# Two operand sums cut when they are made, and residual and SBUF corrections added by accumulating DMAs, in the MLP of a hybrid decoder block on one core

## The chip, the cores and the metric

The kernel runs on one core of a Trainium2 chip. The metric is the device time of one execution in microseconds (us), as the median of three runs. PE is the matrix engine, DVE the vector engine, ACT the scalar engine, POOL and SP issue DMAs here. The granted clock is the share of its full 2.4 GHz that TensorE was allowed in a stretch; its other level is 1.2 GHz.

## The reference, cut to what matters

```
h = x + mixer_block(rmsnorm(x))              # S5 branch and short convolution, gated, projected
xn = rmsnorm(h)                              # xn: 1024 features x 1024 positions
a = relu(xn @ w_ff1)                         # 4096 features
h = h + (a * a) @ w_ff2                      # the squared-ReLU MLP
return rmsnorm(h)
```

All is float32. The change touches only the MLP and the residual sum of its last line.

## The kernel before, in words

**Products.** Each float32 operand is cut into a high part (ACT copies it to fp32r) and a low part (DVE subtracts the high part), and a product is three matmuls: high by high, high by low, low by high. Both layers of the MLP are mostly done in groups of seven products (Strassen's scheme in Winograd's form) in place of eight. `seven(g, after)` (L1196) is one group: chains P1, then P4 of the group before (`last_product`, L1243), P5, P2, P6, P3, P7, each of 12 matmuls. Its four results come out of the chains P2 (c11), P3 (c12), P7 (c22) and, a group later, P4 (c21); `done` (L1231) takes them out of PSUM. P4 continues the accumulation in the bank `seed` in which P7 ended, so it can't start before DVE has read c22 from that bank. c12 and c22 each need a correction, `v2` and `s5`, which ACT copies out of PSUM in the middle of the group.

**Stages.** 14 groups of W1 (g = 0 to 13), 16 plain products `pf` of W2 (slab 6), 12 groups of W2 (g = 14 to 25: three chunks q of four groups e), then the last slab of W2 in plain products with the last normalisation.

**Operands of W2.** From g = 2 on each W1 group computes its activations c11, c12, c22, c21 and the sums that the scheme needs of them: t1, t3, n2, t4. POOL stores them to DRAM (`xd`), 256 KB each, seven per group. Before the W2 chunk that needs them, SP loads them (`x_load`, L1177: two loads of 512 KB for each of seven operands B11, t1, B21, n2, B22, t3, t4) and `x_cut` (L1185) cuts each load, with a 128x1024 copy on ACT and a 128x1024 subtraction on DVE (recorded at L930).

**Weights.** `group_load` loads two blocks per group; `w_parts` makes sums (s1, s2 on DVE), highs (h0 to h3 on ACT) and lows (l0 to l3 on DVE). The plan `FIRST` (L1073, W1) or `SECOND` (W2) says behind which chain, `after(i)`, each is written.

**Order.** The order of every engine's queue is the order of the code: what `after(i)` writes stands behind chain i's evacuation. A late instruction holds up all behind it on its engine. SP runs its loads in order, POOL its stores.

**Residual.** `h` after the mixer was stored to DRAM (`hd`, eight blocks of 128x1024). After the W1 groups SP loads the eight blocks into `ha` (L1314), and DVE adds each product of W2 to them: L1330 for `pf`, L1237 in the groups, and a second instruction there, L1239, subtracts v2 or s5.

**End of W2.** During the final group (g = 25) the last slab (`fl`, `slab_cut`) and four weight blocks (`lw`, `cut`) are cut, in turn, at after(2) to after(6).

Of the kernel before, what the change touches and what calls it, by code (L numbers as in the profile page):

```python
# [45 lines left out]
def block_kernel(ctx, tc, x_t, par, ssm, w_u, win, wco, wglu, wo, w1, w2, out):
# [632 lines left out]
    def ssm_z():  # L679
# [34 lines left out]
        (q, nm): dram.tile([P, 4, HALF], F32, tag=f"xd{q}{nm}", name=f"xd{q}{nm}")  # L714
        for q in range(N_CHUNK) for nm in X_OF.values()
# [357 lines left out]
    FIRST = ["s1 h0", "s2 h1 l0", "h2 l1", "l2"], ["", "", "h3", "l3"]  # L1073
# [103 lines left out]
    def x_load(q, name):  # L1177
        ts = []
        for u in range(2):
            t = unit(f"xl{q}{name}{u}", F32R)  # L1180
            nc.sync.dma_start(t.bitcast(F32), xd[q, name][:, 2 * u:2 * u + 2, :].rearrange("p k t -> p (k t)"))
            ts.append(t)
        xq[q, name] = ts
# [15 lines left out]
    def seven(g, after):  # L1199
# [10 lines left out]
        s5, v2 = half(f"s5_{g}"), half(f"v2_{g}")  # L1210
        A.activation(s5, pe, AF.Copy)
# [5 lines left out]
        A.activation(v2, seed, AF.Copy)  # L1217
# [14 lines left out]
    def done(g, quad, ps, less):  # L1232

        i, hh = int(quad[1]) - 1, int(quad[2]) - 1
        if g >= N_GROUP:
            y = h[2 * ((g - N_GROUP) % 4) + i][:, HS[hh]]
            V.tensor_add(y, ps, y)  # L1237
            if less is not None:
                V.tensor_sub(y, y, less)  # L1239
# [4 lines left out]
        def out_of(name, t):  # L1244
            nc.gpsimd.dma_start(xd[q, name][:, c, :], t)
# [74 lines left out]
    for j in range(16):  # L1320
# [10 lines left out]
        if j % 2 and j < 12:
            x_load(0, names_x[j // 2])
            if j > 1:
                x_cut(0, names_x[j // 2 - 1])
# [152 lines left out]
```

## Time and profile before

| | |
|---|---|
| time, median of 3 runs | 1485.74 us (1485.54 to 1486.83) |
| the profiled execution's own time | 1487.28 us |
| its span, first to last instruction | 1485.5 us |
| PE busy | 1450.2 us, 98% of the span |
| DVE busy | 1008.4 us, 68% |
| ACT busy | 545.1 us, 37% |
| POOL busy | 131.3 us, 9% |
| mean granted clock | 0.991 |
| one chain of 12 matmuls, back to back | 2.72 us |
| one group of seven | 19.04 us |

PE is the engine to look at: it has work for nearly the whole span, so time can only be won where it stands idle or where its clock is low. Both happen in few places, so the table of totals says little; the waits of PE say which instruction ended each stop, the timeline says where that instruction stood in its queue, and the windows say what clock followed.

### The profile page before, as it was taken

How to read it: one execution, taken by the hardware profiler on the slowest of the kernel's cores; microseconds unless marked ns; L12 is line 12 of the kernel's file. 1: busy time of each engine (PE TensorE's matmuls, PEld its weight loads, DVE VectorE, ACT ScalarE, POOL GpSimd, SP SyncE). 2: the span in 40 equal slices, each digit the busy share in tenths (PEclk: the TensorE clock that was granted, in tenths of full speed). 3: DMA queues.
4: the chain of work that ended last, by engine and by line, in shares of the span. 5: the costliest groups of instructions: out<-in, count | busy, mean ns of one | idle time of the engine just before them, and what ended most of it. 6: DMA issues, size and time to landing. Idle time of an engine off the chain costs nothing.

```text
span 1485.5 us, 16929 instructions
## 1 busy us (share of the span) xinstructions
PE 1450.2 (98%) x6563; PEld 1200.9 (81%) x6563; DVE 1008.4 (68%) x1573; ACT 545.1 (37%) x776; POOL 131.3 (9%) x306
## 2 busy tenths in 40 slices
PE   9989999999999999999999999999999999998997
PEld 7868888888888888888888878888887787887887
DVE  6678487776877776347536866766666657767565
ACT  6541432223232238324213443333324224344354
POOL 5840000000000000000010001222111000000000
PEclk9999999999999999999999999999999999999999
DMA  5111111101111111114312233444458516162302
GB/s 215 29 43 43 43 43 50 48 32 56 43 43 43 43 43 35 65 57 156 135 43 94 78 105 123 153 156 148 151 169 347 169 53 232 57 217 94 114 28 87
DMA packets 44096, 144.31 MB, mean 97 GB/s; under 512 B 5488, under 2 KB 9968, under 8 KB 44016
## 3 DMA queue, kind: packets, MB, share of 16 engines
q1 hardware_dynamic: 34736, 112.82, 22.6%
q0 software_dynamic: 9280, 30.42, 5.3%
q8 instruction: 51, 0.84, 0.2%
q14 instruction: 29, 0.24, 0.1%
HBM read 108.61 MB, written 34.60 MB: 96 GB/s over the span
## 4 chain that ended last, share of the span: by engine, by line
PE 83%; DVE 9%; ACT 4%; DMA 2%; issue 2%; SPq 0%; DVEq 0%; ACTq 0%
PE ps L134 8%; PE ps L136 8%; PE ps L135 8%; PE seed L1088 4%; PE seed L1090 4%; PE seed L1089 4%; PE pa L1090 3%; PE pa L1089 3%; PE pa L1088 3%; PE pe L1090 3%; PE pe L1089 3%; PE pe L1088 3%; PE pc L134 2%; PE pg L136 2%; PE pg L135 2%; PE pc L136 2%
## 5 line engine op out<-in xcount | busy, mean ns | idle before, releaser
L134 PE MATMUL ps<-xh,wh 128*128 128x512 f32 x656 | 259.8, 396 | 1.2 <-ACT wh L94 1.2
L136 PE MATMUL ps<-xh,wl 128*128 128x512 f32 x656 | 256.1, 390 | 2.2 <-DVE wl L95 2.2
L135 PE MATMUL ps<-xl,wh 128*128 128x512 f32 x656 | 255.3, 389 | 0.0
L136 PEld LDWEIGHTS ps<-xh,wl 128*128 128x128 f32 x656 | 123.1, 188 | 29.8 <-DVE wl L95 3.9
L134 PEld LDWEIGHTS ps<-xh,wh 128*128 128x128 f32 x656 | 123.3, 188 | 28.6 <-ACT wh L94 2.3
L135 PEld LDWEIGHTS ps<-xl,wh 128*128 128x128 f32 x656 | 123.2, 188 | 25.3
L95 DVE TENSOR_TENSOR wl<-wr,wh 128x1024 fp32r<-128x1024 f32 x57 | 70.1, 1230 | 59.0 <-ACT wh L94 59.0
L94 ACT ACTIVATE wh<-wr 128x1024 fp32r<-128x1024 f32 x57 | 59.6, 1047 | 52.3 <-PE pc L135 21.0
L1204 ACT ACTIVATE seed<-pa 128x512 f32<-128x512 f32 x26 | 15.1, 582 | 160.2 <-PE pa L1090 160.2
L893 POOL DMA_DIRECT2D hd<-h x16 | 8.9, 559 | 711.5 <-ACT ssum L895 636.4
L1060 DVE TENSOR_TENSOR gl<-gs,gh 128x1024 fp32r<-128x1024 f32 x52 | 63.3, 1219 | 0.0
L1056 ACT ACTIVATE gh<-gs 128x1024 fp32r<-128x1024 f32 x52 | 54.7, 1052 | 22.5 <-DVE gs L1052 11.7
L134 PE MATMUL pc<-vh,wh 128*128 128x512 f32 x128 | 49.9, 390 | 0.0
L134 PE MATMUL pw<-mh,hwo 128*128 128x512 f32 x128 | 49.9, 390 | 0.0
L136 PE MATMUL pc<-vh,wl 128*128 128x512 f32 x128 | 49.8, 389 | 0.0
L136 PE MATMUL pw<-mh,lwo 128*128 128x512 f32 x128 | 49.8, 389 | 0.0
L135 PE MATMUL pw<-ml,hwo 128*128 128x512 f32 x128 | 49.8, 389 | 0.0
L134 PE MATMUL pg<-zh,wh 128*128 128x512 f32 x128 | 49.8, 389 | 0.0
L135 PE MATMUL pg<-zl,wh 128*128 128x512 f32 x128 | 49.8, 389 | 0.0
L136 PE MATMUL pg<-zh,wl 128*128 128x512 f32 x128 | 49.8, 389 | 0.0
L135 PE MATMUL pc<-vl,wh 128*128 128x512 f32 x128 | 49.8, 389 | 0.0
L1060 DVE TENSOR_TENSOR gl<-rg,gh 128x1024 fp32r<-128x1024 f32 (+1 forms) x52 | 49.5, 952 | 0.0
(518 smaller groups left out, 3565.6 us busy)
## 6 DMA issues: line engine op xcount, KB each, us to landing
rg<-in_w SPq DMA_DIRECT2D x52, 512.0 KB, 3.6
wr<-in_win SPq DMA_DIRECT2D x41, 512.0 KB, 3.5
wr<-in_wco SPq DMA_DIRECT2D x8, 512.0 KB, 3.5
wr<-in_wglu SPq DMA_DIRECT2D x8, 512.0 KB, 3.5
rwo<-in_wo SPq DMA_DIRECT2D x8, 512.0 KB, 6.8
h<-in_x_t SPq DMA_DIRECT2D x8, 512.0 KB, 7.5
hd<-h POOLq DMA_DIRECT2D x16, 256.0 KB, 2.3
fl<-h2d SPq DMA_DIRECT2D x8, 512.0 KB, 4.3
```

What stands on the lines that cost most here:

```text
L94: A.activation(hi, r, AF.Copy)
L95: V.tensor_sub(lo, r, hi.bitcast(F32))
L134: T.matmul(ps, wh[:, j, :], xh[:, cols], start=start and i == 0, stop=False)
L135: T.matmul(ps, wh[:, j, :], xl[:, cols], start=False, stop=False)
L136: T.matmul(ps, wl[:, j, :], xh[:, cols], start=False, stop=stop and i == n - 1)
L893: nc.gpsimd.dma_start(hd[i][:, c], h[i][:, c])
L1056: A.activation(hi[nm], src[nm], AF.Copy)
L1060: V.tensor_sub(lo[nm], src[nm], hi[nm].bitcast(F32))
L1088: T.matmul(p, wh[:, kb, :], xh, start=first and kb == 0, stop=False, skip_group_check=True)
L1089: T.matmul(p, wh[:, kb, :], xl, start=False, stop=False, skip_group_check=True)
L1090: T.matmul(p, wl[:, kb, :], xh, start=False, stop=kb == 3, skip_group_check=True)
L1204: A.activation(seed, pa, AF.Copy, scale=-1.0)
```

## The change

1. **Two sums cut at once.** t1 and n2 are cut into high and low in the W1 group that makes them: ACT copies the 128x512 high, POOL stores it; DVE's subtraction (`rest`) waits in a list and is written at the next `after(i)`, and its store follows. A group has nine stores instead of seven. `x_load` of such a name loads four blocks of 512 KB instead of two, and `x_cut` does nothing for it.
2. **Corrections by DMA.** In W2 groups, ACT copies v2 and s5 with the scale -1, and a POOL DMA adds them to `ha` in SBUF (24 of 256 KB) in place of the subtraction L1239. In W1 groups v2 and s5 lie in one tile of the pool `late`.
3. **Residual by DMA.** The eight loads into `ha` are gone. ACT copies each `pf` product into `ha`, where DVE added it; eight POOL DMAs of 512 KB add `hd` to `ha` during g = 15 and 16.
4. **Another order.** The plan FIRST moves its steps, the weights of g = 0 are all made before its first chain, `group_load(g + 2)` stands two chains later, the loads of slab 6 two chains earlier; the cuts of B22 move from after(6) of the last group of a chunk to after(0) of the next chunk; the four weight cuts of the final group move to its after(6) and behind its last product.

```
+SPLIT = ("t1", "n2")
-    FIRST = ["s1 h0", "s2 h1 l0", "h2 l1", "l2"], ["", "", "h3", "l3"]
+    FIRST = ["", "", "s1 h0", "l0 h1", "l1"], ["s2 h2", "l2", "h3", "l3"]
     def x_load(q, name):
+        for part in "hl" if name in SPLIT else "r":
+            for u in range(2):
+                t = unit(f"x{part}{q}{name}{u}", F32R)
+                src = xd[q, name, part][:, 2 * u:2 * u + 2, :]
+                nc.sync.dma_start(t.bitcast(F32), src.rearrange("p k t -> p (k t)"))
     def x_cut(q, name):
+        if name in SPLIT:
+            return
     def seven(g, after):
-        s5, v2 = half(f"s5_{g}"), half(f"v2_{g}")
-        A.activation(s5, pe, AF.Copy)
+        if g < N_GROUP:
+            sv = late.tile([P, S], F32, tag="l", name=f"sv{g}")
+            s5, v2 = (sv[:, c] for c in HS)
+        else:
+            s5, v2 = half(f"s5_{g}"), half(f"v2_{g}")
+        sign = 1.0 if g < N_GROUP else -1.0
+        A.activation(s5, pe, AF.Copy, scale=sign)
     def done(g, quad, ps, less):
             V.tensor_add(y, ps, y)
             if less is not None:
-                V.tensor_sub(y, y, less)
+                nc.gpsimd.dma_start(y, less, accum_op=ALU.add)
+        def split_out(name, t, lo=None):
+            hi = half(f"h{name}_{g}", F32R)
+            A.activation(hi, t, AF.Copy)
+            out_of(name, hi.bitcast(F32), "h")
+            def rest():
+                V.tensor_sub((t if lo is None else lo).bitcast(F32R), t, hi.bitcast(F32))
+                out_of(name, t if lo is None else lo, "l")
+            waiting.append(rest)
-            out_of("t1", t1)
+            split_out("t1", t1)
-            out_of("n2", n2)
+            split_out("n2", n2, half(f"ln2_{g}"))
         def after(i):                                    # W1 groups
             for prep in preps:
                 next(prep, None)
-            if i == 4 and g + 2 < N_GROUP:
+            while waiting:
+                waiting.pop(0)()
+            if i == 6 and g + 2 < N_GROUP:
                 group_load(g + 2)
-                if i == 2:
+                if i == 0:
                     slab_load(plain_slab)
     for e in range(8):
-        t = late.tile([P, S], F32, tag="l", name=f"ha{e}")
-        nc.sync.dma_start(t, hd[e])
-        V.tensor_add(h[e][:, HS[hh]], p, h[e][:, HS[hh]])
+        A.activation(h[e][:, HS[hh]], p, AF.Copy)
         def after(i):                                    # W2 groups
+            if q == 0 and e in (1, 2) and 1 <= i <= 4:
+                k = 4 * (e - 1) + i - 1
+                nc.gpsimd.dma_start(h[k], hd[k], accum_op=ALU.add)
             if e == 3 and not final:
                 if i != 1:
                     x_load(q + 1, names_x[max(i - 1, 0)])
-                if i >= 3:
+                if i in (3, 5):
                     x_cut(q + 1, names_x[i - 3])
             if final:
-                    if i > 2:
-                        n = 4 * (n_slab - 1) + i - 3
-                        w2p[n] = cut(w2p[n], f"w2_{n}", blocks8)
+                if i == 6:
+                    last_cut(0)
+    for k in range(1, 4):
+        last_cut(k)
```

Three places show the new order. DVE at the end of g = 13, the last W1 group, before (`fl6` are the lows of slab 6, `lw2_24` a weight low, `holda` c12, `holdb` t1, `holdc` c22 read from the bank `seed1`):

```order
L1168 TENSOR_TENSOR fl6_1_8362<-fl6_1_8362,fh6_1_8403 128x1024
L736 TENSOR_TENSOR lw2_24_8409<-rw2_24_8406,hw2_24_8408 128x1024
L1263 TENSOR_TENSOR holda_13_8380<-pe13_8309,v2_13_8356 128x512
L1152 SCALAR_TENSOR_TENSOR holda_13_8380<-holda_13_8380 128x512
L1272 TENSOR_TENSOR holdb_13_8424<-holda_13_8380 128x512
L1168 TENSOR_TENSOR fl6_2_8364<-fl6_2_8364,fh6_2_8429 128x1024
L1263 TENSOR_TENSOR holdc_13_8444<-seed1_6434,s5_13_8355 128x512
```

and in the changed kernel:

```order
L1169 TENSOR_TENSOR fl6_1_8415<-fl6_1_8415,fh6_1_8494 128x1024
L737 TENSOR_TENSOR lw2_24_8500<-rw2_24_8497,hw2_24_8499 128x1024
L1284 TENSOR_TENSOR holda_13_8471<-pe13_8394,sv13_8455 128x512
L1153 SCALAR_TENSOR_TENSOR holda_13_8471<-holda_13_8471 128x512
L1293 TENSOR_TENSOR holdb_13_8515<-holda_13_8471 128x512
L1264 TENSOR_TENSOR holdb_13_8515<-holdb_13_8515,ht1_13_8519 128x512
L1169 TENSOR_TENSOR fl6_2_8417<-fl6_2_8417,fh6_2_8524 128x1024
L1284 TENSOR_TENSOR holdc_13_8539<-seed1_6439,sv13_8455 128x512
```

One subtraction, which takes ACT's `ht1_13`, stands between t1 and the reading of `seed1`.

DVE at the end of g = 17 (chunk q = 0, before q = 1), before (`xl1t1`, `xl1B21`, `xl1n2` are lows of t1, B21 and n2; `ha6` is c12, `ha7` c22 from `seed1`; `gl` and `gs` are weight lows and sums):

```order
L930 TENSOR_TENSOR xl1t10_9234<-xl1t10_9234,xh1t10_9285 128x1024
L930 TENSOR_TENSOR xl1t11_9236<-xl1t11_9236,xh1t11_9287 128x1024
L1060 TENSOR_TENSOR gl3_18_9293<-rg18_0_9174,gh3_18_9266 128x512
L1237 TENSOR_TENSOR ha6_8487<-pe17_9179,ha6_8487 128x512
L1239 TENSOR_TENSOR ha6_8487<-ha6_8487,v2_17_9232 128x512
L930 TENSOR_TENSOR xl1B210_9253<-xl1B210_9253,xh1B210_9313 128x1024
L930 TENSOR_TENSOR xl1B211_9255<-xl1B211_9255,xh1B211_9315 128x1024
L1060 TENSOR_TENSOR gl1_18_9319<-gs1_18_9263,gh1_18_9291 128x1024
L1237 TENSOR_TENSOR ha7_8489<-seed1_6434,ha7_8489 128x512
L1239 TENSOR_TENSOR ha7_8489<-ha7_8489,s5_17_9231 128x512
L930 TENSOR_TENSOR xl1n20_9281<-xl1n20_9281,xh1n20_9339 128x1024
```

and in the changed kernel:

```order
L1061 TENSOR_TENSOR gl3_18_9391<-rg18_0_9270,gh3_18_9366 128x512
L1247 TENSOR_TENSOR ha6_8581<-pe17_9275,ha6_8581 128x512
L931 TENSOR_TENSOR xr1B210_9353<-xr1B210_9353,xh1B210_9411 128x1024
L931 TENSOR_TENSOR xr1B211_9355<-xr1B211_9355,xh1B211_9413 128x1024
L1061 TENSOR_TENSOR gl1_18_9417<-gs1_18_9363,gh1_18_9389 128x1024
L1247 TENSOR_TENSOR ha7_8582<-seed1_6439,ha7_8582 128x512
L931 TENSOR_TENSOR xr1B220_9407<-xr1B220_9407,xh1B220_9456 128x1024
L931 TENSOR_TENSOR xr1B221_9409<-xr1B221_9409,xh1B221_9458 128x1024
L1052 TENSOR_TENSOR gs2_18_9462<-gs1_18_9363,rg18_1_9272 128x512
```

The two lows of t1 and the subtraction of v2_17 no longer stand ahead of `seed1`, and behind it come the lows of B22 instead of s5_17 and n2.

DVE in the final group g = 25, before (`fl7` are lows of slab 7, `lw2_28` to `lw2_31` the lows of the last weights):

```order
L736 TENSOR_TENSOR lw2_28_10386<-rw2_28_10358,hw2_28_10385 128x1024
L1168 TENSOR_TENSOR fl7_2_10317<-fl7_2_10317,fh7_2_10404 128x1024
L736 TENSOR_TENSOR lw2_29_10408<-rw2_29_10360,hw2_29_10407 128x1024
L1237 TENSOR_TENSOR ha6_8487<-pe25_10299,ha6_8487 128x512
L1239 TENSOR_TENSOR ha6_8487<-ha6_8487,v2_25_10356 128x512
L1168 TENSOR_TENSOR fl7_3_10319<-fl7_3_10319,fh7_3_10425 128x1024
L736 TENSOR_TENSOR lw2_30_10429<-rw2_30_10362,hw2_30_10428 128x1024
L1237 TENSOR_TENSOR ha7_8489<-seed1_6434,ha7_8489 128x512
```

and in the changed kernel:

```order
L1169 TENSOR_TENSOR fl7_2_10405<-fl7_2_10405,fh7_2_10488 128x1024
L1247 TENSOR_TENSOR ha6_8581<-pe25_10387,ha6_8581 128x512
L1169 TENSOR_TENSOR fl7_3_10407<-fl7_3_10407,fh7_3_10505 128x1024
L1247 TENSOR_TENSOR ha7_8582<-seed1_6439,ha7_8582 128x512
L737 TENSOR_TENSOR lw2_28_10523<-rw2_28_10446,hw2_28_10522 128x1024
L1247 TENSOR_TENSOR ha7_8582<-seed1_6439,ha7_8582 128x512
L737 TENSOR_TENSOR lw2_29_10540<-rw2_29_10448,hw2_29_10539 128x1024
```

No weight low stands ahead of the reading of `seed1` any more.

## Rows read from the trace of the kernel before

**Rows 1.** Page: engine, busy us (share of the span), instructions.

```profile
PE 1450.2 (98%) x6563; PEld 1200.9 (81%) x6563; DVE 1008.4 (68%) x1573; ACT 545.1 (37%) x776; POOL 131.3 (9%) x306
```

**Rows 2.** Waits of PE: waiter <- releaser: us in total, times, longest us.

```profile
PE seed L1088 <- DVE ha L1237: 6.8, 3, 2.8
PE pa L1090 <- DVE gl L1060: 4.5, 3, 2.1
PE pe L1090 <- DVE gl L1060: 3.4, 1, 3.4
PE seed L1088 <- DVE holdc L1263: 2.6, 1, 2.6
```

**Rows 3.** Windows: stretch, length, busy us of PE, PEld, DVE, ACT, POOL; PEclk; DMA share; GB/s.

```profile
860.00:870.00 10.00, 6.63 (x22) 5.15 (x22) 9.53 (x12) 6.16 (x8) 0.34 (x1) 0.83 0.17 47
...
1120.00:1130.00 10.00, 7.37 (x33) 5.80 (x32) 8.38 (x10) 4.39 (x5) 0.98 (x3) 1.00 1.02 408
...
1180.00:1190.00 10.00, 7.08 (x23) 5.02 (x22) 8.58 (x10) 5.46 (x7) 0.00 (x0) 0.83 0.45 151
...
1260.00:1270.00 10.00, 9.62 (x35) 7.43 (x34) 9.16 (x11) 4.02 (x6) 0.00 (x0) 0.83 0.32 88
...
1340.00:1350.00 10.00, 8.00 (x33) 6.22 (x32) 9.18 (x11) 4.97 (x7) 0.00 (x0) 0.94 0.29 85
1350.00:1360.00 10.00, 10.00 (x40) 8.14 (x40) 7.53 (x10) 3.44 (x4) 0.00 (x0) 0.89 0.10 37
...
1420.00:1430.00 10.00, 10.00 (x60) 9.06 (x61) 3.99 (x7) 2.52 (x6) 0.00 (x0) 0.83 0.00 0
```

**Rows 4.** Timeline (start, length, engine, line, operation) of DVE in g0.

```profile
862.32 1.22 DVE L1060 TENSOR_TENSOR gl<-gs,gh 128x1024 fp32r<-128x1024 f32 x1
```

**Rows 5.** Timeline of DVE and PE, end of g11, a steady W1 group.

```profile
1086.91 0.69 DVE L1272 TENSOR_TENSOR holdb<-holda 128x512 f32<-128x512 f32 x1
1088.11 0.69 DVE L1263 TENSOR_TENSOR holdc<-seed,s 128x512 f32<-128x512 f32 x1 [0.51 <-PE seed L1090]
...
1090.63 0.39 PE L1088 MATMUL seed<-xht,gh 128*128 128x512 f32 x1
```

**Rows 6.** Timeline of DVE, end of g13.

```profile
1126.30 0.69 DVE L1272 TENSOR_TENSOR holdb<-holda 128x512 f32<-128x512 f32 x1
1126.91 1.22 DVE L1168 TENSOR_TENSOR fl<-fl,fh 128x1024 fp32r<-128x1024 f32 x1
1128.04 0.69 DVE L1263 TENSOR_TENSOR holdc<-seed,s 128x512 f32<-128x512 f32 x1
```

**Rows 7.** Timeline of DVE, end of g17.

```profile
1254.58 2.35 DVE L930 TENSOR_TENSOR xl1B<-xl1B,xh1B 128x1024 fp32r<-128x1024 f32 x2
1256.85 1.22 DVE L1060 TENSOR_TENSOR gl<-gs,gh 128x1024 fp32r<-128x1024 f32 x1
1257.98 0.69 DVE L1237 TENSOR_TENSOR ha<-seed,ha 128x512 f32<-128x512 f32 x1
```

**Rows 8.** Timeline of DVE, final group.

```profile
1418.01 1.22 DVE L736 TENSOR_TENSOR lw<-rw,hw 128x1024 fp32r<-128x1024 f32 x1
1419.15 0.68 DVE L1237 TENSOR_TENSOR ha<-seed,ha 128x512 f32<-128x512 f32 x1
```

**Rows 9.** Lines by form, 860 to 1430: count | busy, mean ns | idle before.

```profile
L1056 ACT ACTIVATE gh<-rg 128x512 fp32r<-128x512 f32 x26 | 16.2, 623 | 0.0
...
L1239 DVE TENSOR_TENSOR ha<-ha,v 128x512 f32<-128x512 f32 x12 | 8.3, 692 | 0.9
...
L930 DVE TENSOR_TENSOR xl1t<-xl1t,xh1t 128x1024 fp32r<-128x1024 f32 x6 | 7.1, 1222 | 1.9 <-ACT xh1t L1189 1.9
```

**Rows 10.** DMA issues: queue, count, KB each, median us from issue to landing.

```profile
rg<-in_w SPq DMA_DIRECT2D x52, 512.0 KB, 3.6
...
ha<-hd SPq DMA_DIRECT2D x8, 512.0 KB, 11.0
...
xd0t<-holdb POOLq DMA_DIRECT2D x8, 256.0 KB, 2.8
```

More of the change, by code (lines that the diff above doesn't have):

```diff
@@ L713, in block_kernel @@
     xd = {
-        (q, nm): dram.tile([P, 4, HALF], F32, tag=f"xd{q}{nm}", name=f"xd{q}{nm}")
-        for q in range(N_CHUNK) for nm in X_OF.values()
+        (q, nm, part): dram.tile([P, 4, HALF], F32, tag=f"xd{q}{nm}{part}", name=f"xd{q}{nm}{part}")
+        for q in range(N_CHUNK) for nm in X_OF.values() for part in ("hl" if nm in SPLIT else "r")
     }
@@ L1043, in sums @@
         def sums(nm):
-            t = four(unit(f"gs{nm}_{g}")) if g == 0 else wpool.tile(
+            t = four(unit(f"gs{nm}_{g}")) if g == 0 and nm == "1" else wpool.tile(
                 [P, 8, P], F32, tag="w", name=f"gs{nm}_{g}").rearrange("p (a k) m -> p a k m", a=2)
@@ L1130, in group_first @@
     def group_first():
-        next(prep0)
-        next(prep0)
+        for _ in prep0:
+            pass
     group_load(0)
@@ L1177, in x_load @@
     def x_load(q, name):
[L1178 to L1183, printed above, removed]
+        got = []
+        for part in "hl" if name in SPLIT else "r":
[3 more added lines that the diff above has]
+                nc.sync.dma_start(t.bitcast(F32), src.rearrange("p k t -> p (k t)"))
+                got.append(t)
+        xq[q, name] = got if len(got) == 2 else list(zip(got[:2], got[2:]))
     def x_cut(q, name):
+        if name in SPLIT:
+            return
         ops = []
@@ L1216, in seven @@
         chain(seed, g, "P6", False)
-        A.activation(v2, seed, AF.Copy)
+        A.activation(v2, seed, AF.Copy, scale=sign)
         after(4)
@@ L1242, in done, with out_of @@
         q, c = divmod(g - 2, 4)
-        def out_of(name, t):
-            nc.gpsimd.dma_start(xd[q, name][:, c, :], t)
+        def out_of(name, t, part="r"):
+            nc.gpsimd.dma_start(xd[q, name, part][:, c, :], t)
+        def split_out(name, t, lo=None):
[6 more added lines that the diff above has]
+            waiting.append(rest)
         hold = held.setdefault(g, {})
@@ L1276, in done @@
             V.tensor_sub(t3, hold["a"][:, HS[1]], t)
+            V.tensor_sub(n2, hold["a"][:, HS[0]], t3)
             out_of("t3", t3)
-            V.tensor_sub(n2, hold["a"][:, HS[0]], t3)
-            out_of("n2", n2)
+            split_out("n2", n2, half(f"ln2_{g}"))
         elif quad == "c21":
@@ L1288, in block_kernel @@
         last_g = g == N_GROUP - 1
-        if g == 0:
-            for _ in prep0:
-                pass
         preps = [group_steps(g, 1), group_steps(g + 1, 0) if not last_g else iter(())]
@@ L1308, in block_kernel @@
     last_product(N_GROUP - 1)
+    while waiting:
+        waiting.pop(0)()
     h = []
     for e in range(8):
-        t = late.tile([P, S], F32, tag="l", name=f"ha{e}")
-        nc.sync.dma_start(t, hd[e])
-        h.append(t)
+        h.append(late.tile([P, S], F32, tag="l", name=f"ha{e}"))
     names_x = list(X_OF.values())
@@ L1329, in block_kernel @@
         products(p, w2p[n], range(4 * ii, 4 * ii + 4), slab[plain_slab], HS[hh])
-        V.tensor_add(h[e][:, HS[hh]], p, h[e][:, HS[hh]])
[L1331 to L1334, printed above, removed]
+        A.activation(h[e][:, HS[hh]], p, AF.Copy)
+        if j % 3 == 1:
+            x_load(0, names_x[j // 3])
+        if j % 3 == 0 and 0 < j < 15:
+            x_cut(0, names_x[j // 3 - 1])
         if j >= 10:
@@ L1337, in block_kernel, with last_cut @@
     group_load(g0 + 1)
+    def last_cut(k):
+        n = 4 * (n_slab - 1) + k
+        w2p[n] = cut(w2p[n], f"w2_{n}", blocks8)
     for g in range(g0, g0 + 4 * N_CHUNK):
@@ L1347, in after @@
                     if i == 0:
-                        x_cut(0, "t3")
+                        x_load(0, "t3")
+                        x_cut(0, "B22")
+                    elif i == 1:
                         x_load(0, "t4")
-                    elif i == 2:
-                        x_cut(0, "t4")
                 elif i == 0:
```

8 lines of the change are left out of this document (4 added, 4 removed).

## The prediction

> **What bounds the kernel now.** The page's engine totals come first [rows 1]: PE is busy 98% of the span, DVE 68%. So an instruction taken off DVE is worth nothing by itself; it is worth something where PE waits for DVE. The waits of PE come second [rows 2]: in the stages that the change touches PE stops in four groups of waits, all ended by DVE. Three stops of 6.8 us in all wait for the add L1237 that reads c22 out of `seed` (at P4 of g17, 2.15; of g21, 1.87; of g25, 2.79). Three of 4.5 us wait for a weight low `gl0` (in g14, 2.11; g18, 0.38; g22, 2.00). One of 3.4 us in g0 waits for `gl1`, one of 2.6 us at P4 of g13 for `holdc`. Third the windows, for what a stop costs behind it [rows 3]: after the stops in g0, g14, g17, g21/g22 and g25 the granted clock is 0.83 in a stretch of 10 us (for g22 0.94 and 0.89 in two neighbours), which is half speed (1.2 GHz) for 3.4 us of it. Full-speed work lost: 10 x (1 - 0.83) = 1.7 us each, for g22 10 x (0.06 + 0.11) = 1.7 as well. After the 2.6 us stop of g13 the clock stayed 1.00. Last the timeline, for what stood ahead of the late DVE instruction in its queue [rows 4 to 8].
>
> **g0.** Before, `gl1` starts at 862.32, behind the operand lows of the stage ahead [rows 4], and P5 waits 3.37 us. Now prep0 is made whole in group_first, some 40 us earlier, where s2's place on DVE goes to `l1`. By my count of the tail, s2, h2 and l2 (two sums of 0.69, a low of 1.22) are done at 866, and P3 needs them at 868.2. The stop goes, and its half-speed stretch: -3.4 - 1.7 = **-5.1**. Its cover is the 2.2 us of PE work between 866 and 868.2; were s2 later than that, part of the 3.4 comes back, not more.
>
> **W1 groups 2 to 13.** Each gets two highs on ACT (0.62) and two lows on DVE (0.69) [rows 9]. In a steady group, t1 is made at 1086.91 and c22 read at 1088.11, and P4 starts at 1090.63 [rows 5]. Now t1's rest stands between: 1086.91 + 0.69 (t1) + some 0.75 (the high and two hand-overs) = 1088.4, + 0.69 = 1089.0 to 1089.7 for the start of the c22 read with some scatter in the hand-overs; it lasts 0.69, so P4's 1090.63 is met with 0.2 to 0.9 us to spare. Price nil, cover 0.2 to 0.9 us. The two stores more per group (2 x 256 KB at 2.8 us [rows 10]) leave buffers of which the next user is a group away: nil. The plan's new order gives each low its high a chain ahead; I find no step whose chain comes first: nil.
>
> **g13.** Here P4 follows P7 with no P1 between, so this order costs at once. Before: t1 1126.30, fl 1126.91, c22 read at 1128.04 [rows 6]. Now t1's rest stands behind t1 and needs its high; ACT, in order, makes the next slab high only behind it. So: t1 done 1127.0, high 1127.65, rest to 1128.4, while the slab high ends at 1128.65; its low 1128.65 to 1129.8, c22's read 1129.8 to 1130.5. P7 ends at 1126.15, so the stop is 4.2 to 4.4 us in place of 2.63: +1.6. A stop that long was followed by half speed in every case of [rows 3] but this one of 2.63, so I add 1.7: **+3.3**. Bounds: the read can't end before 0.85 us after P7, which would be -1.8; +3.5 the other way.
>
> **g14.** The lows that stood ahead of `gl0` are of t3, now of B22, as many: the 2.11 us stay, **0**.
>
> **Ends of g17 and g21.** Before g17's c22 add (1257.98) stand, among others, two lows of t1 (2 x 1.14 by their spacing), the subtraction of v2 (0.61) and two of B21 [rows 7, 9]. t1's lows and v2's subtraction are gone, and t1's and n2's highs on ACT. By the same durations B21's lows end at 1254.1 and c22 is read from 1255.3 to 1256.0, ahead of 1256.57 when P4 wants the bank. That stop goes, in both places: -2.15 - 1.87, with a half-speed stretch each (-1.7 x 2). But B22's lows now stand behind it: ACT's highs follow P1's copy (1257.1 to 1259.1), the lows end at 1260.4, s2 at 1261.75, c21's add, then `gl0` from 1262.4 to 1263.6. P2's third matmul wants it at 1262.5: a stop of 1.15 in g18 and g22 instead of 0.38 and 2.00. I take no clock loss for 1.15 us; if there is one, +1.7 each. Together -4.0 - 3.4 - 2.4 + 2.3 = **-7.5**.
> The loads must hold for this: e = 3 now brings 9 MB in some 25 us (7 MB before), and a full queue moved 408 GB/s [rows 3]: by that the 2 MB more are 5 us (an estimate). B22 would land near 1255, needed at 1257.1: cover 2 us.
>
> **g25.** Before, two weight lows stand between c12 and the c22 read at 1419.15 [rows 8]. Now none does, c22 is read as P7 ends (1417.09), and P4 starts 0.85 us later: -2.79 + 0.85 and the half-speed stretch -1.7: **-3.6**. The four weight lows move behind: 1419, 1422.5, 1423.6, 1424.8. The last blocks take them from 1420.6 on at 2.72 us or more apart, cover 1 us or more.
>
> **Corrections and residual by DMA.** 24 subtractions leave DVE (24 x 0.69 [rows 9]); what they are worth is counted above. Each DMA of 256 KB leaves a half tile of which the next user is a group away, and every later reader of those bytes is 2.7 us of PE work or more behind: nil. The residual is harder, for DVE must wait: POOL issues the adds of hd0 to hd7 in order, hd2 behind c11 of g15 (31 us after g14 began, counted in chains of 2.72), and DVE's c12 add of g15, wanted at 35.5, waits for hd2 to land; its c22 read, wanted by 40.9, for hd3; c11 of g16 (49.1) for hd4. Behind that add on DVE stand the weight lows of the next group. No such DMA is in this trace. Nearest rows: a plain 256 KB store by POOL 2.8, a 512 KB load into a free queue 3.6, and 11.0 for the old hd loads in a queue at 1.0 share [rows 10]. Here the queue is nearly free (0.45 at 1180 [rows 3]), so I take 3.6 to 5: **0**. At 10 us each, one behind another, hd3 lands at 31 + 20 = 51 against 40.9: 10 us, and hd4 about 8 more: +18. The eight loads that go, with those of `pf`, take 4 MB out of the full queue behind 1120 [rows 3]; PE didn't wait for them: nil.
> The Trainium skill ("DMA: Bandwidth & Descriptors", "Rules for kernel authors") says that an accumulating DMA reads its destination and writes it later with nothing holding the bytes in between, which speaks against this edit: every other access must wait for its semaphore, DVE's add among them. The same page ("Anatomy of one DMA") fits 2.0 us + bytes / 436e3 for a plain one: 2.6 us for 256 KB (the row has 2.8) and by estimate 3.2 for 512 KB, with no price for the addition; by it the sum would stand at 0 here, by the 11.0 row at some +20.
>
> **Sum.** -5.1 + 3.3 + 0 - 7.5 - 3.6 = -12.9 us. Of the profiled execution's 1487.28 that leaves 1474.4; it lies 1.5 above the median of the runs, so the forecast for the median is 1485.74 - 12.9 = **1472.8**.
>
> **Rivals.**
> (a) Part of it holds: the loads of e = 3 land late, so that g18's and g22's operands bring the stops back (+7.5), or g13 and the 1.15 us stops cost a clock stretch more: about 1477 to 1481. For: the queue was full at 1.02 before [rows 3]. Against: 2 us of cover.
> (b) The stops only change places. DVE's work in e = 3 and e = 0 is then late elsewhere, and the gain of g0 and g25 (8.7) pays for g13 and the residual: 1483 to 1488. For: g13 and the two 1.15 us stops show how it goes. Against: 24 x 0.69 and 8 x 1.22 of lows leave these stages for good.
> (c) Slower, in W1: the hand-over DVE, ACT, DVE for t1 is longer than I count, because ACT stands in another copy; c22's read then misses P4 in all 12 groups. Each stop of 1 us, with up to 1.7 of clock, makes 12 to 32 us, 1485 to 1505. It decides where the hop is more than 1.1 us beyond the cover: 12 x 1.07 = 12.9. Against: in g11 ACT's last copy there (v2) is a chain old.
> (d) Slower, in g15/g16: an accumulating DMA of 512 KB takes over about 8 us, where the +18 at 10 us has grown to the gain: 1486 to 1491.
>
> **How the numbers follow.** My forecast (1468 to 1477) 0.50, (a) 0.20, (b) 0.13, (c) 0.09, (d) 0.08. Range: the forecast's low end less a clock stretch or two, 1466 (g13 at its lower bound -1.8 instead of +3.3 gives 1467.7), up to (b) without its last microsecond, 1487. About 0.2% (3 us) is what a measurement can tell here. Faster holds the forecast, (a) and a third of (b): 0.74; same two thirds of (b) and the low end of (c): 0.11; slower the rest of (c) and (d): 0.15.
>
> **What would show it.** In the profile after: no wait of PE in g0, at P4 of g17 and g21; at P4 of g13 a wait of some 4.3 us with a half-speed window behind it; about 1.1 us for `gl0` in g18 and g22; 0.85 us at P4 of g25; no wait at P4 in g2 to g12; hd adds that land in under 5 us. The forecast is wrong if P4 waits in each W1 group, if DVE idles in g15 for a DMA, or if the x loads of e = 3 release ACT late.

## The result and the profile after

The changed kernel took 1473.1 us (median of 4 runs, 1470.26 to 1473.65) beside 1485.64 for the kernel before: 0.9915 of it, with a 95% interval of 0.9895 to 0.9936. That is 12.5 us less; forecast were 12.9 and a median of 1472.8. A second set of runs gave 0.9906 (0.9888 to 0.9925). The profiled execution took 1473.05 us, its span 1471.3.

The waits of PE, from the two stages that the change touches (waiter <- releaser: us in total, times, longest us):

```profile
PE seed L1089 <- DVE holdc L1284: 4.2, 1, 4.2
PE pa L1091 <- DVE gl L1061: 4.2, 3, 2.1
PE seed L1089 <- DVE ha L1247: 2.2, 2, 1.4
...
PE pa L1089 <- ACT gh L1057: 0.8, 1, 0.8
```

Against [rows 2], `gl1` of g0 (3.4 us) is gone, `holdc` has grown from 2.6 to 4.2, and the three stops for c22 (6.8) have become two of 2.2 in all. One of these is at P4 of g25 (0.78), as forecast, the other at P4 of g15 (1.40), where there was none.

The windows of the places of [rows 3] (stretch, length, busy us of PE, PEld, DVE, ACT, POOL; PEclk; DMA share; GB/s):

```profile
860.00:870.00 10.00, 10.00 (x46) 8.29 (x45) 8.63 (x12) 5.05 (x7) 0.54 (x1) 1.00 0.38 132
...
1120.00:1130.00 10.00, 6.85 (x24) 5.58 (x25) 8.12 (x11) 4.36 (x6) 3.79 (x7) 0.83 0.98 346
...
1180.00:1190.00 10.00, 9.83 (x36) 7.98 (x37) 6.81 (x9) 5.85 (x9) 0.00 (x0) 0.83 0.32 108
...
1210.00:1220.00 10.00, 8.60 (x38) 6.79 (x38) 4.98 (x7) 2.60 (x3) 3.55 (x4) 1.00 0.70 120
...
1260.00:1270.00 10.00, 8.98 (x40) 7.43 (x40) 8.38 (x9) 6.67 (x9) 0.00 (x0) 1.00 0.60 236
...
1340.00:1350.00 10.00, 10.00 (x45) 8.27 (x45) 9.20 (x11) 4.20 (x6) 0.28 (x1) 1.00 0.37 148
...
1410.00:1420.00 10.00, 10.00 (x84) 9.96 (x84) 7.78 (x14) 4.81 (x12) 0.00 (x0) 1.00 0.04 8
```

Half speed is left behind g13 (new) and g14 (as before); behind g0, g17, g21/g22 and g25 the clock is 1.00.

DVE's timeline of the changed kernel at the place of [rows 5], the end of g11 (start, length, line, operation, [idle time before]):

```profile
1079.74 0.69 DVE L1293 TENSOR_TENSOR holdb<-holda 128x512 f32<-128x512 f32 x1
1081.19 0.69 DVE L1264 TENSOR_TENSOR holdb<-holdb,ht 128x512 fp32r<-128x512 f32 x1 [0.76 <-ACT ht L1260]
1081.80 0.68 DVE L1284 TENSOR_TENSOR holdc<-seed,sv 128x512 f32<-128x512 f32 x1
```

The same view at the place of [rows 6], the end of g13:

```profile
1118.88 0.69 DVE L1293 TENSOR_TENSOR holdb<-holda 128x512 f32<-128x512 f32 x1
1120.32 0.69 DVE L1264 TENSOR_TENSOR holdb<-holdb,ht 128x512 fp32r<-128x512 f32 x1 [0.76 <-ACT ht L1260]
1121.27 1.22 DVE L1169 TENSOR_TENSOR fl<-fl,fh 128x1024 fp32r<-128x1024 f32 x1 [0.26 <-ACT fh L1168]
1122.41 0.68 DVE L1284 TENSOR_TENSOR holdc<-seed,sv 128x512 f32<-128x512 f32 x1
```

And at that of [rows 8], the final group:

```profile
1404.33 1.22 DVE L1169 TENSOR_TENSOR fl<-fl,fh 128x1024 fp32r<-128x1024 f32 x1
1406.43 0.69 DVE L1247 TENSOR_TENSOR ha<-seed,ha 128x512 f32<-128x512 f32 x1 [0.89 <-PE seed L1091]
1407.04 1.22 DVE L737 TENSOR_TENSOR lw<-rw,hw 128x1024 fp32r<-128x1024 f32 x1
```

In g11 t1's rest stands ahead of the c22 read, after 0.76 us of waiting for ACT; the read ends at 1082.48, 1 us before P4 (1083.46). In g13 rest and slab low stand ahead of it, and it ends 4.1 us after P7 (1118.98). In g25 it starts as P7 ends.

Laid beside each other matmul by matmul, the two profiled executions differ like this: -1.9 us before 116 us, where the two programs are alike (so that isn't of the change); g0 -5.3; g13 and the first plain product +2.9; g14 and the plain products 0; g15 +1.7; g17/g18 -3.4; g21/g22 -4.7; g25 -3.6.

### The profile page after: what moved, and what is told of

It is laid out like the page before. It is cut to its first block, busy times and chain, and to the rows that moved or that the text cites. A ratio compares the mean times of both kernels' runs of the same rounds, so it can differ in the third digit from the quotient of the medians.

```text
span 1471.3 us, 17088 instructions
## 1 busy us (share of the span) xinstructions
PE 1443.5 (98%) x6563; PEld 1197.6 (81%) x6563; DVE 982.1 (67%) x1545; ACT 557.0 (38%) x804; POOL 171.5 (12%) x362
## 4 chain that ended last, share of the span: by engine, by line
PE 83%; DVE 6%; issue 6%; ACT 4%; DMA 1%; POOL 0%; SPq 0%; DVEq 0%; ACTq 0%; POOLq 0%
PE ps L135 8%; PE ps L137 8%; PE ps L136 8%; PE seed L1089 4%; PE seed L1091 4%; PE seed L1090 4%; PE pa L1091 3%; PE pa L1090 3%; PE pa L1089 3%; PE pe L1091 3%; PE pe L1090 3%; PE pe L1089 3%; PE pc L135 2%; PE pc L136 2%; PE pg L137 2%
## 5 line engine op out<-in xcount | busy, mean ns | idle before, releaser
L1089 PE MATMUL seed<-xht,gh 128*128 128x512 f32 x112 | 44.4, 396 | 4.2 <-DVE holdc L1284 4.2
```

The source lines that it names most:

```text
L1089: T.matmul(p, wh[:, kb, :], xh, start=first and kb == 0, stop=False, skip_group_check=True)
```

## Experiments

Each kernel is the changed one with what its diff shows. Times are medians; "trace" means matmul by matmul against the profiled execution of the changed kernel. Runs of one kernel spread over some 4 us (1469.8 to 1474.0 in the second set of the changed kernel), so a single part's worth is read from stops in its trace first.

**t1 and n2 whole again.**

```
-SPLIT = ("t1", "n2")
+SPLIT = ()
-                if i in (3, 5):
+                if i >= 3:
                     x_cut(q + 1, names_x[i - 3])
```

> The changed kernel, but t1 and n2 are stored whole and cut before each chunk, as in the kernel before. My theory (time is lost only where DVE reaches a reading that PE waits for too late, plus about 1.5 us of half clock behind a long stop): the two lows of t1 (2.3 us) stand ahead of the c22 reads of g17 and g21 again, so P4 stops there for about 1.5 us, and n2's lows put gl0 of g18 and g22 off to stops of about 1.6 us instead of 1.03; with the clock some +3.7 us each place. At the end of g13 the stop shrinks from 4.2 to about 2.6 us without a half-clock stretch, -3. Sum about +4.5 us on the changed kernel, 1477.5. Rival (the amount of DVE work counts): W1 loses 24 lows of 0.69 = 16.6 us, W2 gets 8 of 1.22 = 9.8 back, and the time falls below 1473.

Measured 1472.74 us (1470.95 to 1475.71), ratio to the kernel before 0.9914 (0.9896 to 0.9932): no change. The stop of g13 is 2.38 us (still with half speed), P4 of g17 and g21 stop for 1.13 each, `gl0` of g18 and g22 for 1.29 instead of 1.03. That is +1.4 us of stops at each place (+1.6 in the trace), not +3.7, with no half speed behind it, against 1.6 less in g13 and 1.2 less at g15, where the stop varies by itself (see the changed kernel again, below). The mechanism held, its size was half; the rival's amount of work made no gain either. So the 0 in the median is a sum: cutting t1 and n2 early brings 3.3 us at the ends of g17 and g21 and costs 1.6 in g13.

**Corrections by DVE.**

```
-        sign = 1.0 if g < N_GROUP else -1.0
+        sign = 1.0
-                nc.gpsimd.dma_start(y, less, accum_op=ALU.add)
+                V.tensor_sub(y, y, less)
```

> The changed kernel, but in the W2 groups DVE subtracts v2 and s5 again and the 24 accumulating DMAs are gone. My theory: only two places feel it, g18 and g22, where the subtraction of s5 stands ahead of gl0: stops of 1.65 instead of 1.03 us; the c22 reads of g17 and g21 are just met (0.6 us of cover gone). +1.3 us, with half-clock stretches +4.7: 1474.4 to 1477.8. Rival (the amount counts): 24 x 0.69 = 16.6 us come back, 1489.7.

Measured 1472.06 us (1470.35 to 1474.21), 0.991 (0.9892 to 0.9928): 24 subtractions more on DVE cost nothing. In the trace g17/g18 and g21/g22 take as long as in the changed kernel, to 0.1 us, and the stop at P4 of g15 is gone (-1.7), with `hd` landing in 7.6 us (median) where no corrections go by DMA. The stops for `gl0` didn't grow; they are 0.64, since P4 ahead of them starts 0.4 us later. DVE's timeline at g17/g18 says why. The changed kernel:

```profile
1252.98 0.68 DVE L1247 TENSOR_TENSOR ha<-seed,ha 128x512 f32<-128x512 f32 x1
1255.67 2.36 DVE L931 TENSOR_TENSOR xr1B<-xr1B,xh1B 128x1024 fp32r<-128x1024 f32 x2 [2.01 <-ACT xh1B L1194]
...
1259.76 1.21 DVE L1061 TENSOR_TENSOR gl<-rg,gh 128x1024 fp32r<-128x1024 f32 x1
```

The same place with the corrections by DVE:

```profile
1251.40 0.68 DVE L1247 TENSOR_TENSOR ha<-seed,ha 128x512 f32<-128x512 f32 x1
1252.12 0.69 DVE L1249 TENSOR_TENSOR ha<-ha,s 128x512 f32<-128x512 f32 x1
1253.61 2.36 DVE L931 TENSOR_TENSOR xr1B<-xr1B,xh1B 128x1024 fp32r<-128x1024 f32 x2 [0.80 <-ACT xh1B L1194]
...
1257.69 1.21 DVE L1061 TENSOR_TENSOR gl<-rg,gh 128x1024 fp32r<-128x1024 f32 x1
```

The subtraction of s5 fills DVE's wait for ACT's high of B22 (2.01 us idle, now 0.80). In both `gl0` starts 4.1 us behind B22's lows.

**The residual by loads.**

```
-        h.append(late.tile([P, S], F32, tag="l", name=f"ha{e}"))
+        t = late.tile([P, S], F32, tag="l", name=f"ha{e}")
+        nc.sync.dma_start(t, hd[e])
+        h.append(t)
-        A.activation(h[e][:, HS[hh]], p, AF.Copy)
+        V.tensor_add(h[e][:, HS[hh]], p, h[e][:, HS[hh]])
-                nc.gpsimd.dma_start(h[k], hd[k], accum_op=ALU.add)
```

> The changed kernel, but the residual comes by eight loads ahead of the plain products and DVE adds the products to it, as before; no accumulating DMA of hd. My theory: the stop of 1.40 us at P4 of g15, which ends with an hd DMA (7.8 us to land), goes; the loads that fill the queue behind 1110 hold up nothing that PE waits for: -1.4 to -1.7 us, about 1471.5. Rival (taking 4 MB out of the full queue was part of the gain): slower than 1473 by some us, with stops in g13 or among the plain products.

Measured 1473.26 us (1471.95 to 1475.09), 0.9916 (0.99 to 0.9932): no change, made of several that cancel. The stop of g15 is gone (trace -1.7). But P4 of g13 stops for 5.2 us, in the waits of PE:

```profile
PE seed L1089 <- DVE holdc L1284: 5.2, 1, 5.2
PE pa L1091 <- DVE gl L1061: 4.2, 3, 2.1
```

ACT's timeline ahead of it:

```profile
1114.87 0.60 ACT L1281 ACTIVATE rc<-pa 128x512 f32<-128x512 f32 x1 [3.75 <-DMA xd2n2h<-hn]
1115.37 1.05 ACT L1168 ACTIVATE fh<-fl 128x1024 fp32r<-128x1024 f32 x1
```

ACT's copy of c11 waits 3.75 us for a buffer that a POOL store (`xd2n2h`) still reads; the loads fill the DMA engines (share 1.02 between 1110 and 1120; 0.78 in the changed kernel), slab highs and lows come later, and the stop is 1.0 longer. P4 itself takes 0.8 more, for the clock is low for longer behind the stop (0.70 between 1120 and 1130, 0.83 in the changed kernel's first profile, 0.68 in its second, so that isn't of the loads): +1.8. So taking the loads out of that queue was worth 1 us, which I had put at nothing. It is worth that only with t1 and n2 cut early: the store that ACT waits for is n2's high, and in the two runs with whole sums ACT's copy of c11 waits for PE alone and the stop is 2.38, with the loads (the order alone, below) and without.

**The residual's adds later.**

```
-            if q == 0 and e in (1, 2) and 1 <= i <= 4:
-                k = 4 * (e - 1) + i - 1
+            if g0 < g <= g0 + 4 and i in (1, 3):
+                k = 2 * (g - g0 - 1) + i // 2
```

> The changed kernel, but the adds of hd2 to hd7 are issued one to two groups later (hd2, hd3 in g16, hd4, hd5 in g17, hd6, hd7 in g18), each after its group's own adds. My theory: no DVE add waits for an hd DMA any more, the stop at P4 of g15 goes, -1.4 to -1.7 us, about 1471.5. Rival: the slow DMAs themselves hold POOL's queue and the corrections behind them, and a stop of the same size shows in g16 to g18.

Measured 1478.65 us (1476.55 to 1482.7), 0.9953 (0.9934 to 0.9971): 5.5 us slower, against both. No stop in g15, but, by the waits of PE, in g17 and g18:

```profile
PE pa L1091 <- DVE gl L1061: 5.5, 3, 2.3
PE seed L1089 <- DVE ha L1247: 4.3, 2, 3.5
```

DVE's timeline there:

```profile
1249.84 1.23 DVE L931 TENSOR_TENSOR xr1B<-xr1B,xh1B 128x1024 fp32r<-128x1024 f32 x1 [2.52 <-ACT xh1B L1194]
1252.49 1.23 DVE L931 TENSOR_TENSOR xr1B<-xr1B,xh1B 128x1024 fp32r<-128x1024 f32 x1 [1.42 <-ACT xh1B L1194]
...
1254.77 0.68 DVE L1247 TENSOR_TENSOR ha<-seed,ha 128x512 f32<-128x512 f32 x1
1260.09 2.50 DVE L931 TENSOR_TENSOR xr1B<-xr1B,xh1B 128x1024 fp32r<-128x1024 f32 x2 [4.64 <-ACT xh1B L1194]
```

DVE waits 2.5, 1.4 and 4.6 us for ACT's highs of B21 and B22, and ACT for their loads:

```profile
1259.00 1.06 ACT L1194 ACTIVATE xh1B<-xr1B 128x1024 fp32r<-128x1024 f32 x1 [6.06 <-DMA xr1B<-xd1B22r]
```

The adds of hd4 and hd5 are in flight among the 9 MB of g17, and the loads of B21 land 13.0 us after their issue and those of B22 14.3 (medians; 6.9 and 9.8 in the changed kernel). P4 stops for 3.47 us and `gl0` for 2.31, each with half speed behind it. This is rival (a) of the prediction, made to happen: the cover of those loads is real and small.

**The order alone.** The three edits above at once: whole sums, corrections by DVE, residual by loads.

> The changed kernel with only its order left: t1 and n2 whole, corrections by DVE, residual by loads and DVE, all as before; the plan of the weights, prep0, the cuts of B22 and the weight cuts of the final group as in the changed kernel. Theory after the first runs (each of the three named parts is worth nothing or next to it, the order carries the gain): stops of about 2 us at P4 of g17 and g21 and of about 1.2 for gl0 (+1 to +2 us each place on the changed kernel), the stop of g13 at 2.6 to 3.5, none at g15: 1474 to 1477. Rival (the three parts carry the gain in W2 together, since each alone is covered by the others): both stops of g17 and g21 come back whole with half-clock stretches, 1479 to 1482.

Measured 1479.11 us (1474.46 to 1481.37), 0.9948 (0.9931 to 0.9966). The rival was right, by the waits of PE:

```profile
PE pa L1091 <- DVE gl L1061: 6.1, 3, 2.1
PE seed L1089 <- DVE ha L1247: 4.5, 3, 1.9
PE seed L1089 <- DVE holdc L1286: 2.4, 1, 2.4
```

DVE's timeline at the end of g17:

```profile
1243.90 2.36 DVE L931 TENSOR_TENSOR xr1t<-xr1t,xh1t 128x1024 fp32r<-128x1024 f32 x2
...
1247.50 0.69 DVE L1249 TENSOR_TENSOR ha<-ha,v 128x512 f32<-128x512 f32 x1
1248.11 2.35 DVE L931 TENSOR_TENSOR xr1B<-xr1B,xh1B 128x1024 fp32r<-128x1024 f32 x2
...
1251.52 0.68 DVE L1247 TENSOR_TENSOR ha<-seed,ha 128x512 f32<-128x512 f32 x1
```

P4 of g17 and g21 stops for 1.87 us, `gl0` for 2.00 and 1.97, with half speed behind both places, as in the kernel before. t1's lows, then v2's subtraction, then B21's lows stand ahead of the read. Singly undone, t1's lows cost 1.13 us there and v2's subtraction 0.4, and the clock held; together they cost 1.87, `gl0` has grown to 2.00, and half speed is back. With the runs above this makes a table of four, the time that one of these ends (g17/g18, g21/g22) takes more than in the changed kernel, in us by the traces (the residual's loads, in the last of the four, change nothing there by themselves; 1.7 of the 4.7 is half speed):

```
                        corrections by DMA   corrections by DVE
t1 and n2 cut early            0                   0.0
t1 and n2 whole               +1.6                +4.7
```

So cutting t1 and n2 early is enough by itself at these ends, the corrections by DMA alone bring 3.1 of the 4.7, and the two together no more than the first: each covers for the other. By the medians the order gives some 8 us and the three parts the other 5 to 6. By place, the order's gain is that of g0 and g25. The list of changes says more of it than holds: at the ends of g17 and g21 the kernel before had the same order, for it cut n2, not B22, at after(6) of a chunk's last group, and B22 at after(0) of the next chunk already. Only for chunk 0 did cuts and loads move, to later plain products and into g14. That is why the stops come back here. In the traces 3.3 of the order's 8 us lie ahead of 116 us, in parts that are alike; from g0 on it is 4.8.

**The weight cuts of the final group put back.**

```
-                if i == 6:
-                    last_cut(0)
+                if i > 2:
+                    last_cut(i - 3)
-    for k in range(1, 4):
-        last_cut(k)
```

> The changed kernel, but the four weight cuts of the final group stand at its after(3) to after(6) again. Theory: two weight lows stand ahead of the c22 read again, the subtraction of v2 doesn't: the stop at P4 of g25 is 2.1 us instead of 0.78, +1.4, with a half-clock stretch +3.1: 1474.5 to 1476.2. Rival (the subtraction was what made it late): no change, 1473.1.

Measured 1472.94 us (1472.74 to 1473.48), 0.9913 (0.9899 to 0.9927); P4 of g25 stops for 2.06 us, trace +1.3, no half speed behind it. The stop is the expected one; in the median it doesn't show. It stays below the 2.79 us of the kernel before, which had v2's subtraction in that place too.

**The plan of the weights put back** (FIRST, prep0 and the place of `group_load` as in the kernel before).

```
-    FIRST = ["", "", "s1 h0", "l0 h1", "l1"], ["s2 h2", "l2", "h3", "l3"]
+    FIRST = ["s1 h0", "s2 h1 l0", "h2 l1", "l2"], ["", "", "h3", "l3"]
-            if i == 6 and g + 2 < N_GROUP:
+            if i == 4 and g + 2 < N_GROUP:
```

> The changed kernel, but the plan FIRST, the place of prep0 and of the weight loads in the W1 groups are those of before. Theory: P5 of g0 stops for gl1 for 3.4 us with a half-clock stretch behind it, +5.1, and nothing in the other W1 groups: 1478.2. Rival (the plan is what lets the W1 groups bear t1's and n2's cuts): besides that, P4 or P3 stops in some of the 12 groups, and the time is above 1483.

Measured 1476.58 us (1474.2 to 1478.81), 0.9936 (0.992 to 0.9951). The stop of g0 is back, alone, with its half speed, trace +5.3 there, 3.5 in the median; its row in the waits of PE:

```profile
PE pe L1091 <- DVE gl L1061: 3.4, 1, 3.4
```

and the window behind it:

```profile
860.00:870.00 10.00, 8.54 (x31) 6.89 (x32) 8.39 (x11) 5.25 (x8) 0.00 (x0) 0.83 0.19 55
```

No other W1 group stops, so the plan's new order is not what lets them bear t1's and n2's cuts.

**c22 read first in g13.** ACT makes the last two slab highs at after(5); DVE makes their lows and t1's rest behind the c22 read.

```
+            if not last_g or i == 6:
+                if last_g:
+                    slab_low(plain_slab, 2)
+                    slab_low(plain_slab, 3)
                 while waiting:
                     waiting.pop(0)()
-                elif 3 <= i:
+                elif 3 <= i < 5:
                     slab_cut(plain_slab, i - 3)
+                elif i == 5:
+                    slab_high(plain_slab, 2)
+                    slab_high(plain_slab, 3)
```

> The changed kernel, but in g13 ACT makes the last two slab highs together and DVE reads c22 ahead of the last two slab lows and of t1's rest. Theory: the stop at P4 of g13 falls from 4.2 to about 1.2 us and has no half-clock stretch behind it: -3.0 - 1.4, 1468.7. Rival (the stop only moves): the first plain product waits for the slab lows, and the time stays at 1473.

Measured 1466.29 us (1463.72 to 1469.39), 0.987 (0.9851 to 0.9889). P4 of g13 stops for 1.25 us, the clock stays 1.00, the plain product doesn't wait; trace -4.3 there (the medians, of two sets, differ by 6.8).

**A version better than both: that, and B22 and t3 cut behind the weights' steps.**

```
+            if e == 0 and i in (1, 2):
+                x_cut(q, ("B22", "t3")[i - 1])
```

(behind the steps of `preps`, in place of the cuts at after(0) and ahead of them at after(2))

> The changed kernel with two further orders: g13 as in the run that reads c22 first (1466.3), and the cuts of B22 and t3 at the start of each chunk written behind the steps of the weights, so that s2, gh0 and gl0 stand ahead of B22's lows. Theory: the stops in g14 (0.8 + 2.1 us, with a half-clock stretch) and those of gl0 in g18 and g22 (1.03 to 1.08 each) go: -2.9 - 1.5 - 2.1 from 1466.3, some 1460. Rival (the operands are then late): P3 stops for B22 or for l2 in g14, g18, g22, and the time stays at 1464 to 1467.

Measured 1458.77 us (1457.69 to 1459.63), 0.9815 (0.98 to 0.983) of the kernel before, against 0.9906 (0.9888 to 0.9925) for the changed kernel in the same set. The stops of g14, g18 and g22 are gone, and with them the half speed of g14, and so is that of g15, which hangs on `hd` and not on these orders; in these stages PE waits twice, by its waits:

```profile
PE seed L1089 <- DVE holdc L1291: 1.2, 1, 1.2
...
PE seed L1089 <- DVE ha L1254: 0.8, 1, 0.8
```

**The same with the corrections by DVE.**

> As the run before it, with the corrections by DVE instead of 24 accumulating DMAs. Theory: P4 of g17 and g21 stops for 0.4 us each, and the stop at P4 of g15 (0.5 to 1.4 us where the corrections go by DMA) is gone: the same time within 1 us, 1460. Rival (accumulating DMAs cost more than the one stop, since they fill the DMA engines): 2 us or more faster than the run before it.

Measured 1461.04 us (1460.69 to 1462.0), 0.9832 (0.9817 to 0.9846): 2.3 us slower than the run above, as neither the theory nor its rival had it; the executions of the two don't overlap, the intervals of the ratios just do. The trace shows P4 of g17 and g21 0.4 us late each and a stop of 0.55 at P4 of g14. Here the accumulating DMAs are worth a little, since DVE is next to the path at three places.

**The residual's DMAs without the addition.**

```
-                nc.gpsimd.dma_start(h[k], hd[k], accum_op=ALU.add)
+                nc.gpsimd.dma_start(h[k], hd[k])
```

> The changed kernel, but POOL's eight DMAs of hd copy instead of adding: the kernel leaves out the sum of the residual and the products before it, so its time says only what the addition in a DMA costs. Theory A (the addition makes a DMA slow): the eight land in 3 to 5 us (7.8 with the addition, by the tile's row), the DMA engines are busy for less at more GB/s, no stop at P4 of g15, -1.4. Theory B (they are slow because they meet SP's loads and each other): 7 to 9 us as now, 1473.

One run, 1470.1 us, no stop in g15. DVE's add of c12 in g15 waits for PE alone:

```profile
1207.44 0.69 DVE L1247 TENSOR_TENSOR ha<-pe,ha 128x512 f32<-128x512 f32 x1 [2.82 <-PE pe L1091]
```

The eight DMAs land in 5.9 us instead of 8.9 (medians). The last four are issued closer together here, so the four of g15 compare better: 3.5 to 5.1 us instead of 5.9 to 9.7. POOL issues one of these in 0.54 to 0.58 us instead of 0.87 or more, and the DMA engines are little more than half as busy for as many bytes. The window from 1200 to 1210 in the changed kernel:

```profile
1200.00:1210.00 10.00, 10.00 (x45) 8.29 (x45) 3.54 (x5) 2.66 (x4) 2.64 (x3) 1.00 0.95 194
```

and in this one:

```profile
1200.00:1210.00 10.00, 10.00 (x46) 8.29 (x45) 4.41 (x6) 1.94 (x3) 2.00 (x3) 1.00 0.54 202
```

Theory A holds: the addition makes the DMA slow, by some 3 us of landing and nearly twice the engine time, and the four of g15 lie in its 3 to 5; only the median of all eight is above.

**The changed kernel again.**

> The changed kernel itself, beside the others on the same chip: 1473 by all theories; the stop at P4 of g15, 1.40 us in its first profile, differs from run to run if it hangs on the landing of the hd DMAs.

Measured 1471.49 us (1469.83 to 1473.99). The stop of g15 is 0.64 us here, 1.40 in its first profile; `hd` lands in 8.6 us (median). So the stop hangs on the DMAs and not on the order, and the first profile had the longest of those in the table. The clock differs too: it is low for longer behind g13 (0.68 between 1120 and 1130, 0.83 in the first profile) and 1.00 behind the same stops of g14.

The stops of PE, in us, by place ("." is none of 0.3 or more):

```
                 g0    g13   g14        g15   P4 g17/g21    gl0 g18/g22   g25
before           3.37  2.63  0.81+2.11  .     2.15 / 1.87   0.38 / 2.00   2.79
changed          .     4.17  0.81+2.11  1.40  .             1.03 / 1.03   0.78
changed again    .     4.17  0.80+2.12  0.64  .             1.05 / 1.05   0.78
whole sums       .     2.38  0.80+2.12  .     1.13 / 1.13   1.29 / 1.29   0.78
corrections DVE  .     4.17  0.81+2.11  .     .             0.64 / 0.63   0.78
residual loads   .     5.18  0.81+2.11  .     .             1.05 / 1.05   0.78
adds later       .     4.17  0.81+2.11  .     3.47 / .      2.31 / 1.05   0.79
order alone      .     2.38  0.81+2.11  .     1.87 / 1.87   2.00 / 1.97   0.78
weight cuts back .     4.17  0.81+2.11  0.53  .             1.05 / 1.08   2.06
plan back        3.36  4.11  0.81+2.11  .     .             1.03 / 1.05   0.79
read first       .     1.25  0.81+2.11  0.70  .             1.08 / 1.08   0.78
better version   .     1.25  .          .     .             .             0.78
```

## Why the prediction came true, and where it didn't

- **g0, -5.1:** -5.3 in the trace, +5.3 when put back. Right, clock included.
- **W1, nil:** right. The c22 read started 3.51 us after c12 (1081.80 - 1078.29); I had 3.54 to 4.2. It leaves 1 us, g1 to g12 take as long as before in the trace, and rival (c) never came near.
- **g13, +3.3:** a stop of 4.17 and a window at 0.83: +2.9. Right, but in part by luck: I had put the added stores and the loads that go at nothing, and with the stores and the loads the stop is 5.18. The run that reads c22 first gave the 2.9 back and 1.4 more.
- **g14, 0:** the stops are right to the hundredth, 0.81 + 2.11.
- **Ends of g17 and g21, -7.5:** -8.1. The stops of 1.15 were 1.03, without clock loss. The place and the wait are right, the credit isn't. I credited the cuts and the subtractions with their sum, step by step; by the table of four the cuts are enough alone, and the subtractions' going adds nothing to them. The subtraction of s5 was worth nothing, for DVE idles 2 us there for ACT. Nor is it new that B22's lows stand behind the c22 read: they did so before, behind n2's.
- **g25, -3.6:** -3.6. The order alone has v2's subtraction and the same 0.78 us; with the weight cuts put back and no subtraction it is 2.06, without half speed. So moving the cuts suffices, and by itself the subtraction's going takes 0.7 us off the stop; that no half speed followed in that one profile can't be laid to it, since behind stops of that size it comes and goes (last section).
- **Corrections and residual, 0:** the step that failed. I took 3.6 to 5 us for an accumulating DMA of 512 KB, by the rows of plain transfers; the median of the eight was 8.9, and hd2 and hd3, on which g15 waits, took 7.8 and 9.7. As plain copies the four of g15 do land in 3.5 to 5.1, so the term was sized for the wrong operation. In DVE's timeline of g15 the add of c12 stands idle for 6.42 us until hd2 has landed (2.82 of them it waits for PE in any case), the read of c22 0.64 for hd3:

```profile
1212.47 0.69 DVE L1247 TENSOR_TENSOR ha<-pe,ha 128x512 f32<-128x512 f32 x1 [6.42 <-DMA ha<-hd]
...
1214.93 0.69 DVE L1247 TENSOR_TENSOR ha<-seed,ha 128x512 f32<-128x512 f32 x1 [0.64 <-DMA ha<-hd]
```

  That made the stop of 1.40 us (+1.7 in the trace), and it is one of the signs by which I had said that the forecast would be wrong: DVE idle in g15 for a DMA. In the six other profiles with these adds and corrections it is 0.70 at most, so 1.40 is its upper end. It is rival (d) in kind, but its price was wrong as well: at 8.9 us each I had +8 for hd3 alone, counting the DMAs one behind another, and they overlap. The ends (3.6 and 11.0) held the duration; the value that I chose was the row nearest by size, where the operation was another.
- **The loads that go, nil:** wrong by the other sign; they are worth 1.0 us of the stop in g13 (5.18 against 4.17), where ACT waits for a buffer that one of the added stores still reads. I had put those stores at nothing too.
- **The sum:** -12.9 forecast, -12.5 by the medians, -12.4 by the trace from g0 on. The misses are small and of both signs, and that is luck: +1.7 at g15, against -0.2 in g0, -0.4 in g13 and -0.6 at the ends of g17 and g21.
- The clock's part, four stretches gone and one new: right in this trace; in the changed kernel's second profile the one behind g14 is gone and the one behind g13 longer.
- The Trainium skill ("DMA: Bandwidth & Descriptors", "Rules for kernel authors") asks that another access of the same bytes wait for the semaphore of an accumulating DMA. The trace shows what that wait costs (3.6 of DVE's 6.42 us); no run here shows what comes of leaving it out. The fit that the Trainium skill gives for a plain one (same page, "Anatomy of one DMA") makes an estimated 3.2 us for 512 KB. That is just below the 3.5 to 5.1 of the four copies of g15 and far below the 5.9 to 9.7 with the addition: the measurement decides.

## What to carry to other kernels

Work taken off an engine is worth what stands between it and the instruction that the bottleneck waits for; undo each part alone and all at once, since parts that cover each other look worthless singly (here 0 each by the medians, and 5 to 6 us together), and read the result by place, since a 0 can be a gain here and a loss there. Ahead of a reading that frees the bank for the next product, or of a low that it needs, put nothing that can stand behind it: two such moves took the changed kernel from 1471.5 to 1458.8 us in one set of runs. An accumulating DMA isn't a free add: it fills the DMA engines for longer, and the next access waits for its landing.

## What the hardware showed that I had not expected

- An accumulating DMA of 512 KB from DRAM to SBUF landed in 8.9 us (median of eight; the four of g15 in 5.9 to 9.7, as copies in 3.5 to 5.1); between 1200 and 1210 the DMA engines were 0.95 busy at 194 GB/s with the addition and 0.54 busy at 202 GB/s without. POOL's issue took about 0.87 us (256 KB in SBUF too) instead of 0.54 to 0.58.
- A stop of PE between 2.0 and 2.8 us is followed by half speed in some executions and not in others: 2.63 in g13 of the kernel before wasn't, 2.38 in the run with whole sums was, 2.06 in g25 with the cuts put back wasn't. The same stops of 0.81 and 2.11 in g14 were in the changed kernel's first profile and weren't in its second. All stops above 3 us in the MLP were (3.4, 3.5, 4.2, 5.2). What decides between them stays open.
